# Seven-product groups in eight blocks of the mixers, and another order of pairs in the first down block

## The chip, the cores and the metric

The kernel runs on one core of one Trainium2 chip. TensorE (PE in the profile) multiplies matrices from on-chip memory (SBUF) into the accumulators (PSUM); VectorE (DVE) and ScalarE (ACT) prepare its operands and work on its results; SyncE (SP) issues most of the loads. The metric is the device time of one execution in microseconds (us), the median of several runs.

## The reference, cut to what matters

One decoder layer for 256 tokens of width 2048, all in fp32:

```
h = LN(alpha * x + 0.5 * swiglu(x, w_ffn1_gu, w_ffn1_down))
rq, rk, rv, rg, aq, ak, av, gate_r, gate_a = split(h @ w_in)
ro  = group_norm(retention(rotary(rq), rotary(rk), rv))
ret = (silu(rg) * ro) @ w_ret_out
att = sliding_window_attention(rotary(aq), rotary(ak), av, sinks) @ w_att_out
mixed = (sigmoid(gate_r) * ret + sigmoid(gate_a) * att) @ w_mix_out
h = LN(alpha * h + mixed)
h = LN(alpha * h + 0.5 * swiglu(h, w_ffn2_gu, w_ffn2_down))
out = LN(alpha * h + sigmoid(h @ w_ple_gate) * (p @ w_ple_proj))
```

`swiglu(x) = (silu(g) * u) @ w_down` with `g, u` the two halves of `x @ w_gu`; the inner width is 5632.

## The kernel before, in words

**Products.** Every fp32 operand is kept as a high part (fp32r, the copy of ScalarE) and a low part (the difference, by VectorE): `split`, L83. A product of two operands is three matmuls (L324 to L326): low by high, high by high, high by low. The 256 tokens are two halves t of 128; the weights come in pairs of 128-row slices (`Unit`, one pair p of one block b of 1024 columns, which are two halves c of 512). A **plain pair** ("P") is 2 slices x 2 token halves x 2 column halves, eight products and thus 24 matmuls of 512 columns. A group of seven (`Seven`, "S", L153) gets the same eight block products out of seven, 21 matmuls: it multiplies sums and differences of the blocks. For that VectorE and ScalarE make sums of the weight blocks (`u`, `hu`, `lu`) beside three of the blocks themselves (`hb`, `lb`), L166 to L191; `seven_forms` (L383) makes sums of the left operand's blocks once per input; and four of the seven products are gathered over all sevens of a block in two more PSUM tiles (`aux`, L365), which `seven_common` (L399) folds after the last seven into a tile `eve` that is then added to the sums in PSUM.

**Order.** TensorE, VectorE, ScalarE and the queue of SyncE each run in the order in which the program issues. `plan` lists all weight units in the order of use. A small planner keeps a model clock for TensorE and VectorE (`clock`, `spend`, `after`, L196 to L260) and issues loads and splits of coming units ahead of their use as far as a budget of slots allows: all working tiles share 23 slots (`SLOTS`), `weights(n)` (L260) says how many of them weights may take at that point. A plain unit takes one slot loaded, two more while it is made, two when made; a seven takes one, five more, and keeps four, until `done` (L256). Other work, as the attention's heads, is put in the list `side` and issued piece by piece between units by `run_side` (L267); `lazy` is the same for the rotary tables.

**Stages.** `ffn` (L665) runs the gate and up products in eleven blocks `f1g` (each with four or three sevens but the first), then two down blocks: `f1d` (first 1024 columns) and `f1e`. Its 22 pairs are two per group of four 128-row slices; groups 6 to 9 (`SEVEN_DOWN`) have their forms made. In the first down block all pairs come in the order 0 to 21, with sevens at 12, 14, 15, 16, 18 and 19 (`down_units`, L646; `before_unit` L760 converts the rows for coming groups). In the second, plain pairs and sevens alternate. `Norm` (L461) runs the layer norm in pieces between the last products of one stage (`held`) and the first of the next (`front`), as `EVENTS` lists them: c columns, m moments, s scale, t turn (transposes and split, L485). `mixers` (L852) runs blocks `w_rv` 0, the rotary features `rqk`, `w_rv` 1, `rg` 0 and 1, the features `aqk` and `av`, then `gr` 0 and 1, `ga` 0 and 1, then for each b `w_ret` and `w_att`, and last `w_mix` 0 and 1; all these blocks are plain. The retention's heads, two at a time, go through `side` in steps `ret1` (scores), `ret2` (products and statistics), `ret2b` (normalization and gate), `ret3` (transposes) and `ret3b` (split). The attention's heads do so in `att1`, `att1b`, `att1c`, `att2`, `att3`, in four steps each beside `gr` and `ga`.

Of the kernel before, what the change touches and what calls it, by code (L numbers as in the profile page):

```python
# [15 lines left out]
P = 128  # L16
# [24 lines left out]
SEVEN_BOTH = (7, 9)  # L41
# [11 lines left out]
        "a6": "c0 m0 s00", "b6": "t00 c1 m1 s10", "c4": "s01", "c6": "t10", "d1": "s11", "d4": "t01", "d7": "t11",  # L53
    },
    {
        "a6": "c0 m0 s00", "b6": "t00 c1 m1 s10", "c4": "s01", "c6": "t10", "d1": "s11", "d4": "t01", "d7": "t11",
# [9 lines left out]
def layer(ctx: ExitStack, tc: tile.TileContext, io):  # L66
# [200 lines left out]
    def run_side(n=1):  # L267
        for _ in range(n):
            if side:
                side.pop(0)()  # L270
        for _ in range(6):
            if lazy and next(lazy[0], "end") == "end":
                lazy.pop(0)
# [76 lines left out]
    def block(name, b, units, lhs, forms, sums, fold, before=None):  # L350
        sevens = [p for kind, p in units if kind == "S"]
        aux = None
        for j, (kind, p) in enumerate(units):
# [27 lines left out]
            run_side()  # L381
# [79 lines left out]
    class Norm:  # L461
# [23 lines left out]
        def turn(self, t, g):  # L485
# [18 lines left out]
        def vectors_and_p(self):  # L504
            self.vectors = ln_vectors(self.i)
            if self.i < 2:
                self.p = slot([P, 2, 512], F32R, "pt")
                split(self.p[:, :, :S], self.p[:, :, S:], p_raw)

        def held(self, name, b, ps, lhs):  # L510
            self.new = big.tile([P, KD, 512], F32R, tag="ht", name=f"ht{self.i}")
            us = [take(name, b, p) for p in ps]
            for j in range(2 * len(ps)):
                at = j % len(ps)
                some_products(us[at], ps[at], lhs, self.sums, (0,), (j // len(ps),))
                fill()
                run_side()
                self.at("a", j + 1)
# [61 lines left out]
    trig = []  # L580
# [14 lines left out]
    def rotary_tables():  # L595
# [6 lines left out]
        table = slot([P, 8, S], F32, "trig")  # L602
        trig.extend(table[:, j, :] for j in range(4))
        cos_r, sin_r, cos_a, sin_a = trig
        for inv, sgn, cos, sin, nm in ((0, 2, cos_r, sin_r, "r"), (1, 3, cos_a, sin_a, "a")):
# [25 lines left out]
            act.activation(cos, na, AF.Sin)  # L631
            yield
# [4 lines left out]

    def gu_units(j):
        if j == 0:
            return plain(PAIRS)  # L640
        order = "PPSSPSSP" if j % 2 else "PPSPSPSP"
        sevens = list(SEVEN[: order.count("S")])
        rest = [p for p in range(PAIRS) if p not in sevens]
        return [(kind, (sevens if kind == "S" else rest).pop(0)) for kind in order]

    def down_units():  # L646
        first = []
        for g in range(KF // 4):
            first += [("S" if g in SEVEN_DOWN else "P", 2 * g), ("S" if g in SEVEN_BOTH else "P", 2 * g + 1)]
# [15 lines left out]
    def ffn(name, i, ht, norm, keep, residual, keepers, away):  # L665
# [93 lines left out]

        def before_unit(u):  # L760
            g = u // 2 + 2
            others((KF // 4 + min(g, KF // 4 - 1) + 2) // 2 + (1 if u >= 10 else 0))
            if u % 2 == 0:
                if 2 <= u < 2 + 2 * len(SEVEN_DOWN):
                    at = u // 2 - 1
                    r = SEVEN_DOWN[at]
                    made[r] = seven_forms(raws[r // 2][:, r % 2 * 4 : r % 2 * 4 + 4], (space[:, 2 * at], space[:, 2 * at + 1]))
                if g < KF // 4:
                    convert(g)
# [16 lines left out]
        def before_unit(u):  # L786
            others(2 + (4 if u >= 12 else 0) + sum(at >= u for at in last.values()))
# [11 lines left out]
        norm.vectors_and_p()  # L799
        weights(SLOTS - (6 if i else 8))  # L800
# [22 lines left out]

    def plan_mixers():
        plan_block("w_rv", 0, plain(PAIRS))
        plan_features(range(8))
        plan_block("w_rv", 1, plain(PAIRS))
        for b in range(2):
            plan_block("rg", b, plain(PAIRS))
        plan_features(range(16, 21))  # L830
        plan.extend(Columns("w_av", c) for c in range(2))
        for name in ("gr", "ga"):
            for b in range(2):
                plan_block(name, b, plain(PAIRS))
        for b in range(2):
            plan_block("w_ret", b, plain(PAIRS))
            plan_block("w_att", b, plain(PAIRS // 2))
        for b in range(2):
            plan_block("w_mix", b, plain(PAIRS))

    def plain_block(name, b, lhs, n=PAIRS, start=0, sums=None):
        ps = None
        if sums is None:
            ps = [banks(f"{name}{b}{t}") for t in range(2)]
            sums = sums_of(by_half(ps), plain(n))
        block(name, b, plain(n)[start:], lhs, None, sums, None)
        return ps
# [4 lines left out]
    def mixers(ht, norm, residual, keepers, away):  # L852
# [4 lines left out]
        rv = []  # L857

        def values(b, ps):
            after()  # L860
            spend(1024)
            v = slot([P, 2, 1024], F32, f"rvs{b}")
            act.copy(v[:, 0], flat(ps[0]))
            dve.tensor_copy(v[:, 1], flat(ps[1]))
            rv.append(v)

        ps, sums = norm.front("w_rv", 0, rhs, plain(PAIRS))
        lazy.append(rotary_tables())
        plain_block("w_rv", 0, rhs, start=FRONT, sums=sums)
        values(0, ps)  # L870
        assert not lazy
        cos_r, sin_r, cos_a, sin_a = trig
        weights(8)
# [5 lines left out]
        decay = [slot([P, 4, 384], F32, f"dec{j}") for j in range(2)]  # L879
        for j in range(2):  # L880
            act.dma_start(decay[j], io["decay"][:, 4 * j : 4 * j + 4, :])
        values(1, plain_block("w_rv", 1, rhs))
# [5 lines left out]
        def ret1(i):  # L888
            def f():
# [5 lines left out]
                s = slot([P, 2, 384], F32, f"rsc{i}")  # L895
# [29 lines left out]
        def ret2b(i):  # L925
            def f():
# [3 lines left out]
                o = slot([P, 2, 2, DV], F32, f"ron{i}")  # L930
# [9 lines left out]
                keep["o", i] = o  # L940
# [13 lines left out]
        def ret3b(i):  # L954
            def f():
                ps = keep.pop(("r", i))
                ret_t[i] = slot([P, 4, 512], F32R, f"rett{i}")
                spend(256, 256, 256, 256)
                for x in range(4):
                    gk = gn[:, 4 * i + x : 4 * i + x + 1]  # L960
                    hi, lo = ret_t[i][:, x, :S], ret_t[i][:, x, S:]
                    act.mul(hi, ps[:, x], gk)
                    dve.scalar_tensor_tensor(lo, ps[:, x], gk, hi, ALU.mult, ALU.subtract)
            return f

        def gates(b, ps):
            g = slot([P, 2, 1024], F32, f"rgs{b}")
            for t in range(2):
                act.activation(g[:, t], flat(ps[t]), AF.Silu)
            gate.append(g)  # L970

        side.extend([idle] * 5 + [ret1(0), ret1(1), ret2(0)])
        gates(0, plain_block("rg", 0, rhs))
        steps = [
            (ret2b(0), ret2(1)), (ret3(0), ret2b(1)), (ret3b(0), ret3(1)), (ret3b(1),),
            (ret1(2),), (ret1(3),), (ret2(2),), (ret2(3),),
        ]
        both = lambda jobs: lambda: [f() for f in jobs]
        side.extend(both(jobs) for jobs in steps)
        gates(1, plain_block("rg", 1, rhs))  # L980
        side.extend(both(jobs) for jobs in [(ret2b(2),), (ret3(2), ret2b(3)), (ret3b(2), ret3(3)), (ret3b(3),)])
        aq, akv = slot([P, 8, S], F32, "aq"), slot([P, 4, S], F32, "akv")
# [111 lines left out]
        for m in range(8):  # L1094
            side.append(att1(m))
            side.append(both([att1b(m)] + ([att3(m - 1)] if m else [])))
            side.append(att1c(m))
            side.append(att2(m))
        sig = {}
        for name in ("gr", "ga"):  # L1100
            for b in range(2):
                if (name, b) == ("ga", 1):
                    run_side(1)
                ps = plain_block(name, b, rhs)
                sig[name, b] = slot([P, 2, 1024], F32, f"sig{name}{b}")
                for t in range(2):
                    act.copy(sig[name, b][:, t], flat(ps[t]))
        side.append(att3(7))
        run_side(len(side))
# [3 lines left out]

        def quarter(v):
            return lambda k: (v[k // 4][:, k % 4, :S], v[k // 4][:, k % 4, S:])
# [12 lines left out]
        for b in range(2):  # L1128
            pair = sig["gr", b], sig["ga", b]
            for v in pair:  # L1130
                act.activation(v, v, AF.Sigmoid)
            for v, name, n, a in ((pair[0], "w_ret", PAIRS, ret_t), (pair[1], "w_att", PAIRS // 2, att_t)):
                ps = plain_block(name, b, quarter(a), n)
                after()
                spend(1024, 1024)
                for t in range(2):
                    dve.tensor_tensor(v[:, t], v[:, t], flat(ps[t]), ALU.mult)
            v = pair[0]
            spend(1024, 1024)
# [237 lines left out]
```

## Time and profile before

| what | us |
|---|---|
| median of 3 runs | 2305.69 |
| lowest, highest run | 2305.38, 2306.9 |
| the profiled execution | 2308.07 |
| its span, first to last instruction | 2306.3 |

The profile is of one execution, whose own time is 2308.07 us. The page gives each engine's busy time, the chain of work that ended last, and the costliest groups of instructions with what ended the idle time ahead of them. In names of groups, `f1d<-hf_down,f1ac` means that the tile `f1d` is written from `hf_down` and `f1ac`. Matmuls overlap, so that their durations add up to more than TensorE's time.

### The profile page before, as it was taken

To read this page: it belongs to the slowest core of one execution; us is meant where nothing else is said; L and a number is where in the kernel's file an instruction comes from. 1 tells how busy PE (TensorE), PEld (TensorE's weight loads), DVE (VectorE), ACT (ScalarE), POOL (GpSimd) and SP (SyncE) were. 2 spreads that over 40 slices of the span, in tenths; PEclk is the share of its full clock that TensorE was granted. 3 is DMA by queue.
4 is the path that set the end of the run, shared out by engine and by line. 5 is a ranking of instruction groups with operands and counts; after the bars stand their busy time and mean duration, and the time that the engine had idled before them with its cause. 6 is when DMAs were issued, how large, how long until landed. Compare 5 with 4: busy or idle time off the path is not lost.

```text
span 2306.3 us, 26593 instructions
## 1 busy us (share of the span) xinstructions
PE 2275.3 (99%) x10490; PEld 1885.7 (82%) x10490; DVE 1802.4 (78%) x1571; ACT 1128.9 (49%) x922; POOL 0.7 (0%) x6
## 2 busy tenths in 40 slices
PE   8999999999999999999999999999999999999997
PEld 6888888888788888888777888878888888878876
DVE  6999898888988774567555555689989989889876
ACT  5555554555554343344444543356455456555541
POOL 0000000000000000000000000000000000000000
PEclk9999999999999999999999999999999999999999
DMA  8665565655577555445455656676656556455761
GB/s 311 206 199 187 192 209 183 201 201 183 219 262 279 189 201 192 146 164 186 161 164 172 211 201 224 212 238 201 201 179 222 183 175 232 159 205 214 287 261 55
DMA packets 227692, 465.31 MB, mean 202 GB/s; under 512 B 16624, under 2 KB 89072, under 8 KB 225008
## 3 DMA queue, kind: packets, MB, share of 16 engines
q1 hardware_dynamic: 225552, 459.86, 58.3%
q10 hardware_dynamic: 2016, 3.76, 0.5%
q8 instruction: 82, 1.34, 0.2%
q14 instruction: 42, 0.34, 0.0%
HBM read 455.17 MB, written 8.39 MB: 201 GB/s over the span
## 4 chain that ended last, share of the span: by engine, by line
PE 94%; DVE 3%; DMA 1%; issue 1%; ACT 0%; SPq 0%; DVEq 0%; ACTq 0%
PE f1g L326 5%; PE f1g L324 5%; PE f1g L325 5%; PE f2g L324 4%; PE f2g L325 4%; PE f2g L326 4%; PE rqk L288 3%; PE aqk L288 2%; PE f2d L324 1%; PE f2d L325 1%; PE f2d L326 1%; PE ga L324 1%; PE f1e L326 1%; PE f1e L325 1%; PE f1e L324 1%; PE gr L324 1%
## 5 line engine op out<-in xcount | busy, mean ns | idle before, releaser
L85 DVE TENSOR_TENSOR lf_gu<-rf_gu,hf_gu 128x2048 fp32r<-128x2048 f32 (+1 forms) x109 | 239.9, 2228 | 49.6 <-ACT hf_gu L84 48.9
L84 ACT CAST hf_gu<-rf_gu 128x2048 fp32r<-128x2048 f32 (+1 forms) x109 | 200.2, 1861 | 37.4 <-DMA rf_gu<-in_f_gu 15.6
L324 PE MATMUL f1g<-hf_gu,xt 128*128 128x512 f32 x424 | 166.7, 393 | 6.8 <-ACT hf_gu L84 6.4
L326 PE MATMUL f1g<-lf_gu,xt 128*128 128x512 f32 x424 | 166.4, 392 | 1.6 <-DVE lf_gu L85 1.6
L325 PE MATMUL f1g<-hf_gu,xt 128*128 128x512 f32 x424 | 166.4, 392 | 0.0
L188 DVE TENSOR_TENSOR luf_gu<-uf_gu,huf_gu 128x2048 fp32r<-128x2048 f32 x70 | 160.0, 2286 | 1.6
L85 DVE TENSOR_TENSOR lf_down<-rf_down,hf_down 128x2048 fp32r<-128x2048 f32 x60 | 136.4, 2288 | 25.1 <-ACT hf_down L84 18.2
L324 PE MATMUL f2g<-hf_gu,ht 128*128 128x512 f32 x360 | 140.1, 389 | 0.4 <-DVE eve L407 0.4
L326 PE MATMUL f2g<-lf_gu,ht 128*128 128x512 f32 x360 | 140.1, 389 | 0.0
L325 PE MATMUL f2g<-hf_gu,ht 128*128 128x512 f32 x360 | 140.1, 389 | 0.0
L176 ACT CAST huf_gu<-uf_gu 128x1024 fp32r<-128x1024 f32 x70 | 73.7, 1053 | 128.4 <-DVE uf_gu L175 103.4
L84 ACT CAST hf_down<-rf_down 128x2048 fp32r<-128x2048 f32 x60 | 113.8, 1910 | 44.0 <-DMA rf_down<-in_f_down 22.8
L185 DVE TENSOR_TENSOR lbf_gu<-rf_gu,hbf_gu 128x1536 fp32r<-128x1536 f32 x70 | 122.7, 1752 | 13.2 <-ACT hbf_gu L174 13.1
L174 ACT CAST hbf_gu<-rf_gu 128x1536 fp32r<-128x1536 f32 x70 | 103.5, 1479 | 22.3 <-DMA rf_gu<-in_f_gu 17.5
L324 PEld LDWEIGHTS f1g<-hf_gu,xt 128*128 128x128 f32 x424 | 80.5, 190 | 24.3 <-ACT hf_gu L84 6.8
L326 PEld LDWEIGHTS f1g<-lf_gu,xt 128*128 128x128 f32 x424 | 80.4, 190 | 19.0 <-DVE lf_gu L85 2.3
L325 PEld LDWEIGHTS f1g<-hf_gu,xt 128*128 128x128 f32 x424 | 80.3, 189 | 16.7
L175 DVE TENSOR_TENSOR uf_gu<-rf_gu 128x1024 f32<-128x1024 f32 x70 | 85.4, 1219 | 3.7 <-PE f1g L326 1.4
L181 ACT CAST huf_gu<-uf_gu 128x1024 fp32r<-128x1024 f32 x70 | 73.7, 1052 | 25.9 <-DVE uf_gu L180 25.9
L324 PEld LDWEIGHTS f2g<-hf_gu,ht 128*128 128x128 f32 x360 | 67.6, 188 | 14.9 <-issue 0.8
L326 PEld LDWEIGHTS f2g<-lf_gu,ht 128*128 128x128 f32 x360 | 67.6, 188 | 14.1
L727 ACT ACTIVATE eve<-eve 128x1024 f32<-128x1024 f32 x20 | 21.2, 1062 | 118.1 <-DVE eve L725 118.1
(938 smaller groups left out, 6071.9 us busy)
## 6 DMA issues: line engine op xcount, KB each, us to landing
rf_gu<-in_f_gu SPq DMA_DIRECT2D x210, 512.0 KB, 5.7
rf_down<-in_f_down SPq DMA_DIRECT2D x176, 512.0 KB, 4.5
rf_gu<-in_f_gu SPq DMA_DIRECT2D x280, 256.0 KB, 4.3
rw_rv<-in_w_rv SPq DMA_DIRECT2D x32, 512.0 KB, 4.5
rrg<-in_w_in_f SPq DMA_DIRECT2D x32, 512.0 KB, 4.9
rgr<-in_w_in_f SPq DMA_DIRECT2D x32, 512.0 KB, 4.6
rga<-in_w_in_f SPq DMA_DIRECT2D x32, 512.0 KB, 4.7
rw_ret<-in_w_ret SPq DMA_DIRECT2D x32, 512.0 KB, 4.7
```

The source lines that it names most:

```text
L84: act.copy(dst_hi, src)
L85: dve.tensor_tensor(dst_lo, src, dst_hi, ALU.subtract)
L174: act.copy(hb, raw[:, 1:])
L175: dve.tensor_tensor(u[:, 0:2], raw[:, 1:3], raw[:, 0:1].broadcast_to([P, 2, 512]), ALU.add)
L176: act.copy(hu[:, 0:2], u[:, 0:2])
L181: act.copy(hu[:, 2:], u[:, 2:])
L185: dve.tensor_tensor(lb, raw[:, 1:], hb, ALU.subtract)
L188: dve.tensor_tensor(lu, u, hu, ALU.subtract)
L288: pe.matmul(ps[:, f], u.tile_of(kk)[0][:, f * P : (f + 1) * P], rhs(k), start=k == 0, stop=k == KD - 1,)
L324: pe.matmul(o, al, bh, start=first, stop=False)
L325: pe.matmul(o, ah, bh, start=False, stop=False)
L326: pe.matmul(o, ah, bl, start=False, stop=self.left == 0)
```

## The change

- In the mixers eight blocks get sevens (`MIXERS`): four each in `w_rv` 1 and `rg` 0, three each in `gr` 0, `gr` 1, `w_ret` 0 and `w_ret` 1, two each in `w_mix` 0 and 1. `rg` 1, `ga`, `w_att` and `w_rv` 0 stay plain. The forms of the mixers' input come from a kept copy that the first norm now makes too; `ret3b` and `turned` write an fp32 copy first, from which high part, low part and forms are made.
- The blocks come in another order: `gr` 0, `w_ret` 0, `gr` 1, `w_ret` 1, `ga` 0, `ga` 1, `w_att` 0, `w_att` 1.
- The retention's steps of two heads are joined: `ret2` and `ret2b` in one, `ret3`, the next `ret1` and `ret3b` in one. The attention's heads take two steps each instead of four, beside `w_ret` 1 and `ga`.
- In the first down block of both half-FFNs the pairs come in another order (`FIRST_ORDER`), the same six sevens between plain pairs; rows of a group are converted up to five units ahead (`AHEAD`).
- In the norms the second half of the columns is turned earlier or later by one to two products (`EVENTS`), and the split reads PSUM directly, with the kept copy after it.
- Side work is not issued while a block's sevens are under way, and not after a block's last unit; budgets of slots change with all this.

```diff
+FIRST_ORDER = (0, 1, 2, 3, 4, 5, 6, 12, 7, 13, 14, 8, 15, 9, 16, 17, 10, 18, 11, 19, 20, 21)
+FIRST_SEVENS = (12, 14, 15, 16, 18, 19)
+AHEAD = 5
+MIXERS = {
+    ("w_rv", 1): ("PSPSPSSP", (0, 1, 2, 3)),
+    ("rg", 0): ("PSPSPSSP", (0, 1, 2, 3)),
+    ("gr", 0): ("PPSPSPSP", (0, 1, 2)),
+    ("gr", 1): ("PPSPSPSP", (0, 1, 2)),
+    ("w_ret", 0): ("PPSPSPSP", (0, 1, 2)),
+    ("w_ret", 1): ("PPSPSPSP", (0, 1, 2)),
+    ("w_mix", 0): ("PPPPSPSP", (4, 5)),
+    ("w_mix", 1): ("PSPSPPPP", (4, 5)),
+}
...
-        "a6": "c0 m0 s00", "b6": "t00 c1 m1 s10", "c4": "s01", "c6": "t10", "d1": "s11", "d4": "t01", "d7": "t11",
+        "a6": "c0 m0 s00", "b6": "t00 c1 m1 s10", "c5": "t10", "c6": "s01", "d1": "s11", "d4": "t01", "d5": "t11",
...
-                run_side()
+                if (aux is None or not sevens) and j < len(units) - 1:
+                    run_side()
...
-            if self.keep is not None and k0 < 8:
-                full = self.keep[:, k0 : k0 + nk, t * P : (t + 1) * P]
-                act.copy(full, ps)
-                ps = full
             dst = self.new[:, k0 : k0 + nk, :]
             split(dst[:, :, t * P : (t + 1) * P], dst[:, :, S + t * P : S + (t + 1) * P], ps)
+            if self.keep is not None and k0 < 8:
+                act.copy(self.keep[:, k0 : k0 + nk, t * P : (t + 1) * P], ps)
...
         def before_unit(u):
...
+            while todo and firsts[groups.index(todo[0])] <= u + AHEAD:
+                g = todo.pop(0)
+                if g in SEVEN_DOWN:
+                    at = SEVEN_DOWN.index(g)
+                    to = space[:, 2 * at], space[:, 2 * at + 1]
+                    made[g] = seven_forms(raws[g // 2][:, g % 2 * 4 : g % 2 * 4 + 4], to)
+                convert(g)
+            left = {g // 2 for g in todo}
+            others(len(left) + len(groups) - len(todo) + 1 + (1 if u >= 10 else 0))
...
+    def mixers_block(name, b, lhs, forms=None, n=PAIRS, fold=None):
+
+        ps = [banks(f"{name}{b}{t}") for t in range(2)]
+        units = mixers_units(name, b, n)
+        got = []
+        block(name, b, units, lhs, forms, sums_of(by_half(ps), units), lambda *a: got.append((fold or seven_common)(*a)))
+        return ps, got[0] if got else None
+
+    def joined(ps, e, name):
+        if e is None:
+            v = slot([P, 2, 1024], F32, name)
+            for t in range(2):
+                act.copy(v[:, t], flat(ps[t]))
+            return v
+        v = e.rearrange("p (t c) n -> p t (c n)", t=2)
+        after()
+        spend(1024, 1024)
+        for t in range(2):
+            dve.tensor_tensor(v[:, t], v[:, t], flat(ps[t]), ALU.add)
+        return v
...
+            if grp == 4:
+                to = [slot([P, 16, P], F32R, f"hf{w}") for w in "hl"]
+                made["x"] = seven_forms(norm.keep, to)
...
+        def retention(j):
+            i = 2 * j
+            side.append(ret1(i))
+            side.append(both(ret2(i), ret2b(i)))
+            side.append(both(ret3(i), ret1(i + 1), ret3b(i)))
+            side.append(both(ret2(i + 1), ret2b(i + 1)))
+            side.append(both(ret3(i + 1), ret3b(i + 1)))
+            if not j:
+                side.append(retention_forms)
+        weights(10)
+        for b in range(2):
+            load_decay(b)
+            ps, e = mixers_block("rg", b, rhs, forms)
+            v = joined(ps, e, f"rgs{b}")
+            act.activation(v, v, AF.Silu)
+            gate.append(v)
+            retention(b)
+            weights(7)
...
+        weights(8)
+        of_ret = lambda p: made["r"](p)
+        branch = {}
+        for b in range(2):
+            sig = joined(*mixers_block("gr", b, rhs, forms), f"sigr{b}")
+            act.activation(sig, sig, AF.Sigmoid)
+            if b:
+                side.append(both(att1(0), att1b(0)))
+                side.append(att1c(0))
+            ps, e = mixers_block("w_ret", b, quarter(ret_t), of_ret)
+            after()
...
+        for m in range(1, 8):
+            side.append(both(att2(m - 1), att1(m), att1b(m)))
+            side.append(both(att3(m - 1), att1c(m)))
+        side.append(att2(7))
         side.append(att3(7))
-        run_side(len(side))
+        sig = [joined(*mixers_block("ga", b, rhs, forms), f"siga{b}") for b in range(2)]
+        run_side(len(side) - 1)
+        for v in sig:
+            act.activation(v, v, AF.Sigmoid)
...
+            g = 2 * b + hf
+            raw = slot([P, 4, S], F32, f"mixr{g}")
+            act.copy(raw, ps)
             after(clock["pe"] + 1.2)
             spend(1024)
-            split(mt[:, :, :S], mt[:, :, S:], ps)
+            split(mt[:, :, :S], mt[:, :, S:], raw)
+            if any(2 * g in MIXERS[key][1] for key in MIXERS if key[0] == "w_mix"):
+                hl = slot([P, 2, 8, P], F32R, f"mixf{g}")
+                made["m", g] = seven_forms(raw, (hl[:, 0], hl[:, 1]))
```

More of the change, by code (lines that the diff above doesn't have):

```diff
@@ L517, in held @@
                 run_side()
+                if j == 1 and self.i < 2:
+                    self.p = slot([P, 2, 512], F32R, "pt")
+                    split(self.p[:, :, :S], self.p[:, :, S:], p_raw)
                 self.at("a", j + 1)
@@ L636, in plain, with in_order @@
         return [("P", p) for p in range(n)]
+    def in_order(order, sevens):
+        rest = [p for p in range(PAIRS) if p not in sevens]
+        sevens = list(sevens)
+        return [(kind, (sevens if kind == "S" else rest).pop(0)) for kind in order]
     def gu_units(j):
@@ L641, in gu_units @@
         order = "PPSSPSSP" if j % 2 else "PPSPSPSP"
-        sevens = list(SEVEN[: order.count("S")])
-        rest = [p for p in range(PAIRS) if p not in sevens]
-        return [(kind, (sevens if kind == "S" else rest).pop(0)) for kind in order]
+        return in_order(order, SEVEN[: order.count("S")])
     def down_units():
-        first = []
-        for g in range(KF // 4):
-            first += [("S" if g in SEVEN_DOWN else "P", 2 * g), ("S" if g in SEVEN_BOTH else "P", 2 * g + 1)]
+        first = [("S" if p in FIRST_SEVENS else "P", p) for p in FIRST_ORDER]
         rest = [p for p in range(KF // 2) if p // 2 not in SEVEN_DOWN]
@@ L822, in plan_features, with mixers_units, blocks @@
         plan.extend(Columns("f", (grp, c)) for grp in grps for c in range(2))
+    def mixers_units(name, b, n=PAIRS):
+        return in_order(*MIXERS[name, b]) if (name, b) in MIXERS else plain(n)
     def plan_mixers():
-        plan_block("w_rv", 0, plain(PAIRS))
+        def blocks(*which):
+            for name, b in which:
+                plan_block(name, b, mixers_units(name, b, PAIRS // 2 if name == "w_att" else PAIRS))
+        blocks(("w_rv", 0))
         plan_features(range(8))
-        plan_block("w_rv", 1, plain(PAIRS))
-        for b in range(2):
-            plan_block("rg", b, plain(PAIRS))
+        blocks(("w_rv", 1), ("rg", 0), ("rg", 1))
         plan_features(range(16, 21))
         plan.extend(Columns("w_av", c) for c in range(2))
[L832 to L847, printed above, removed]
+        blocks(("gr", 0), ("w_ret", 0), ("gr", 1), ("w_ret", 1), ("ga", 0), ("ga", 1))
+        blocks(("w_att", 0), ("w_att", 1), ("w_mix", 0), ("w_mix", 1))
+    def mixers_block(name, b, lhs, forms=None, n=PAIRS, fold=None):
[16 more added lines that the diff above has]
+        return v
     def flat(ps):
@@ L855, in mixers @@
         both_halves = lambda k: ht[:, k, :]
[L857 to L865, printed above, removed]
+        made = {}
+        forms = lambda p: made["x"](p)
         ps, sums = norm.front("w_rv", 0, rhs, plain(PAIRS))
         lazy.append(rotary_tables())
-        plain_block("w_rv", 0, rhs, start=FRONT, sums=sums)
-        values(0, ps)
-        assert not lazy
+        block("w_rv", 0, plain(PAIRS)[FRONT:], rhs, None, sums, None)
+        rv = [joined(ps, None, "rvs0")]
+        assert "r" in trig_done
         cos_r, sin_r, cos_a, sin_a = trig
-        weights(8)
+        weights(12)
         rq, rk = (slot([P, 8, S], F32, f"r{w}") for w in "qk")
@@ L877, in mixers @@
             features_out(grp, both_halves, ps)
+            if grp == 4:
+                to = [slot([P, 16, P], F32R, f"hf{w}") for w in "hl"]
+                made["x"] = seven_forms(norm.keep, to)
             rotate(ps, f"rr{grp}", (rq, rk)[grp // 4][:, grp % 4 * 2 : grp % 4 * 2 + 2, :], cos_r, sin_r, SH_R)
[L879 to L882, printed above, removed]
+        weights(11)
+        rv.append(joined(*mixers_block("w_rv", 1, rhs, forms), "rvs1"))
         ret_t = {}
@@ L929, in f @@
                 rsqrt(rs, mv[:, :, 1], 4, GN_EPS)
-                o = slot([P, 2, 2, DV], F32, f"ron{i}")
+                o = keep["o", i]
                 spend(*[0] * 10, 256, 256, 256, 256)
@@ L964, in ret3b @@
-            return f
[L966 to L982, printed above, removed]
+                    act.mul(raw[:, x], ps[:, x], gn[:, 4 * i + x : 4 * i + x + 1])
+                after(clock["pe"] + 2)
+                spend(1024)
+                split(ret_t[i][:, :, :S], ret_t[i][:, :, S:], raw)
@@ new lines, in f, with load_decay, retention_forms @@
+                if i == 1:
+                    keep["full"] = keep["raw"]
+            return f
+        both = lambda *jobs: lambda: [f() for f in jobs]
+        decay = []
+        def load_decay(j):
+            decay.append(slot([P, 4, 384], F32, f"dec{j}"))
+            act.dma_start(decay[j], io["decay"][:, 4 * j : 4 * j + 4, :])
+        def retention_forms():
+            to = [slot([P, 16, P], F32R, f"retf{w}") for w in "hl"]
+            made["r"] = seven_forms(keep.pop("full"), to)
@@ L1159, in mixers @@
         ps = [banks(f"mo1{t}") for t in range(2)]
-        sums = sums_of(by_half(ps), plain(PAIRS))
-        plain_block("w_mix", 1, lhs, PAIRS - HELD, sums=sums)
-        norm = Norm(ps, sums, combine, y, stats, 1, LN_EPS, keepers, away)
-        norm.vectors_and_p()
-        weights(15)
-        norm.held("w_mix", 1, range(PAIRS - HELD, PAIRS), lhs)
+        units = mixers_units("w_mix", 1)
+        held = [p for kind, p in units[-HELD:]]
+        sevens = any(kind == "S" for kind, p in units)
+        sums = sums_of(by_half(ps), units)
+        block("w_mix", 1, units[:-HELD], lhs, of_mix, sums, fold(1))
+        norm = Norm(ps, sums, add if sevens else combine, y, stats, 1, LN_EPS, keepers, away)
+        norm.load_vectors()
+        weights(13)
+        norm.held("w_mix", 1, held, lhs)
         return norm
@@ L1194, in embedding @@
         sg = slot([P, 2, 1024], F32, "sg0")
-        plain_block("w_pg", 0, lhs, start=FRONT, sums=sums)
+        block("w_pg", 0, plain(PAIRS)[FRONT:], lhs, None, sums, None)
         whole = slice(0, 1024)
```

112 lines of the change are left out of this document (52 added, 60 removed).

## The prediction, as it was put on record

> **What bounds the kernel now.** I read the page first, then the waits of TensorE, then the stages, then single rows.
>
> ```profile
> span 2306.3 us, 26593 instructions
> PE 2275.3 (99%) x10490; PEld 1885.7 (82%) x10490; DVE 1802.4 (78%) x1571; ACT 1128.9 (49%) x922; POOL 0.7 (0%) x6
> ...
> PE 94%; DVE 3%; DMA 1%; issue 1%; ACT 0%; SPq 0%; DVEq 0%; ACTq 0%
> ```
>
> TensorE is busy for 99% of the span and makes 94% of the chain that ended last. Only fewer matmuls, or fewer of its few waits, can shorten this kernel. The waits of TensorE that touch the change:
>
> ```profile
> PE f_down0s L326 <- DVE luf_down L188: 2.5, 2, 1.2
> PE f_down0s L326 <- DVE lbf_down L185: 2.4, 2, 1.2
> PE f_gu L324 <- DVE ht L85: 1.6, 2, 0.9
> ```
>
> The first two are in the first down blocks (one per half-FFN), the third is where the mixers' norm hands over to the second FFN. A busy TensorE hides the price of one matmul, because starts overlap; so I take it from first and last starts.
>
> ```profile
> L324 PE MATMUL mo<-hw_mix,mixt x64: 389/389/389, 1444.5 to 1487.4; 128*128 128x512 f32 x64
> L326 PE MATMUL mo<-lw_mix,mixt x64: 389/389/393, 1445.0 to 1487.8; 128*128 128x512 f32 x64
> ```
>
> Those 192 matmuls start 191 steps apart over 1487.8 - 1444.5 = 43.3 us: **0.2267 us a matmul**. A plain pair is 24 of them (5.44 us), a seven 21 (4.76 us). The FFN's blocks, which have sevens already, confirm it:
>
> ```profile
> 66.71 0.87 PE f1t L681 x8
> 108.41 0.87 PE f1t L681 x8
> 150.78 0.87 PE f1t L681 x8
> ```
>
> 41.70 us is 180 matmuls (four sevens) plus 0.87 of transposes; 42.37 us is 183 (three) plus 0.87. So a block with sevens has run at TensorE's own pace. By stages (columns: window, length, then busy PE, PEld, DVE, ACT, POOL, clock, DMA):
>
> ```profile
> 60.00:476.70 416.70, 416.31 (x1878) 345.24 (x1877) 379.10 (x275) 229.15 (x179) 0.00 (x0) 1.00 0.62 201
> 476.70:596.50 119.80, 117.32 (x520) 96.38 (x519) 99.06 (x81) 64.41 (x49) 0.00 (x0) 1.00 0.48 171
> 596.50:716.70 120.20, 120.20 (x536) 99.61 (x535) 111.43 (x88) 61.91 (x44) 0.00 (x0) 1.00 0.71 260
> 716.70:853.00 136.30, 136.30 (x734) 118.05 (x733) 101.83 (x122) 53.01 (x40) 0.00 (x0) 1.00 0.57 209
> 853.00:1000.00 147.00, 147.00 (x668) 122.58 (x667) 78.50 (x95) 57.46 (x47) 0.00 (x0) 1.00 0.54 178
> 1000.00:1069.50 69.50, 69.50 (x436) 62.83 (x435) 55.59 (x86) 35.33 (x36) 0.00 (x0) 1.00 0.52 182
> 1069.50:1266.70 197.20, 197.17 (x947) 156.02 (x945) 107.63 (x143) 89.48 (x132) 0.00 (x0) 1.00 0.50 166
> 1266.70:1399.20 132.50, 132.50 (x594) 109.86 (x593) 67.79 (x37) 60.36 (x36) 0.00 (x0) 1.00 0.62 214
> 1399.20:1487.80 88.60, 88.60 (x400) 73.54 (x399) 54.54 (x44) 30.73 (x18) 0.00 (x0) 1.00 0.62 217
> ```
>
> In the FFN, VectorE is 91% busy (379.10 of 416.70) and TensorE loses 0.39 us: that much VectorE work is bearable. The mixers (last six rows) have no TensorE gap to remove, but VectorE is busy for only 465.9 of 771.1 us. That is the room for the new work.
>
> **The change part by part.**
>
> *Sevens in the mixers.* 4+4+3+3+3+3+2+2 = 24 pairs become sevens, each 3 matmuls less: 72 x 0.2267 = **-16.3 us**. The Trainium skill, page "TensorE: Matmul & The Clock Gate", section "Wait — 56ns, not 53.3ns?", has warm N=512 matmuls start 215.7 ns apart; by it the term would be -15.5. The trace has 226.7 ns, and the trace is used.
>
> VectorE pays. One seven, and the plain pair behind it:
>
> ```profile
> 525.53 1.22 DVE L175 TENSOR_TENSOR uf_down<-rf_down 128x1024 f32<-128x1024 f32 x1
> 526.78 0.69 DVE L179 TENSOR_TENSOR uf_down<-rf_down,uf_down 128x512 f32<-128x512 f32 x1
> ...
> 528.12 1.75 DVE L185 TENSOR_TENSOR lbf_down<-rf_down,hbf_down 128x1536 fp32r<-128x1536 f32 x1
> 529.78 2.28 DVE L188 TENSOR_TENSOR luf_down<-uf_down,huf_down 128x2048 fp32r<-128x2048 f32 x1
> 532.01 2.29 DVE L85 TENSOR_TENSOR lf_down<-rf_down,hf_down 128x2048 fp32r<-128x2048 f32 x1
> ...
> 592.98 0.68 DVE L405 TENSOR_TENSOR eve<-eve,f_down0s 128x512 f32<-128x512 f32 x1
> ...
> 594.41 1.22 DVE L407 TENSOR_TENSOR eve<-f_down0s,eve 128x1024 f32<-128x1024 f32 x1
> ```
>
> A seven takes 532.01 - 525.53 = 6.48, a plain pair 2.29: 4.19 more, x24 = 100.6. Each of the eight blocks folds its four common products once (592.98 to 595.63, 2.65): 21. Joining fold and sums is two 1024-wide additions (2 x 1.22, as L407) in six blocks, one of which had a copy: 13; a 2048-wide combine (2.29) in two: 5. Two whole-input forms are four 1024-wide operations and one of 2048 (4 x 1.22 + 2.28 = 7.2): 14; the mix form about 3 (1.22 and four narrow ones). ret3b's sixteen narrow operations become four of 1024: nothing. In all some 157: 465.9 + 157 = 623 of about 755 us, 82%, below the FFN's 91%. So on average TensorE covers this; if the cover went, 157 us would be in the path. ScalarE copies what VectorE subtracts; with as much again (101) on its 326.4 busy it stays under 60%. The 16 grouped sevens load in four DMAs, not two of double the size: the FFN's do so too. The other order of blocks moves loads and matmuls but adds none, and w_ret's rows are ready before the gr blocks. The decay loads move past the features on ScalarE's queue and are used a block later: nothing.
>
> Locally it is tight. Blocks w_rv 1 and rg 0 have four sevens: 4 x 6.48 + 4 x 2.29 + 2.65 + 2.44 = 40.2 of VectorE beside 180 x 0.2267 = 40.8, twice running, without the three-seven block between that relieves the FFN; and the last rotation (five 512-wide operations, 5 x 0.69 as L179) spills in. From w_mix 0's first seven to w_mix 1's last, four sevens and four plain pairs, fold, combine and the norm's sums and statistics (2 x 1.22 and 4 x 0.69 if they run like L407 and L179) are 45 beside 40.8. Three plain pairs made ahead would cover 7 us. I take **+2** (0 to +10).
>
> *Retention.* Before, head products (ret2), normalization (ret2b) and transposes (ret3) stood in three successive side steps; now ret2 and ret2b share one, so one pair, not two, lies between products and transposes. The chain, as it ran:
>
> ```profile
> 942.01 0.59 PE L913 MATMUL ro<-rvs,rsc 128*128 128x256 f32 x2
> ...
> 944.80 0.43 DVE L920 BATCH_NORM_STATS2 gst<-ro 128x6 f32<-128x256 f32 x1 [4.93 <-PE ro L915]
> ...
> 946.87 0.18 DVE L921 BATCH_NORM_AGGREGATE gmv<-gst 128x2 f32<-128x6 f32 x1
> ...
> 949.18 0.16 DVE L413 SCALAR_TENSOR_TENSOR nv<-gmv,cst 128x8 f32<-128x8 f32 x1
> ...
> 951.05 1.65 DVE L936 SCALAR_TENSOR_TENSOR ron<-ro,gmv,rgs 128x256 f32<-128x256 f32 x4
> ...
> 951.56 1.71 ACT L939 ACTIVATE ron<-ron,grs 128x256 f32<-128x256 f32 x4 [6.54 <-DVE ron L936]
> ```
>
> Products and hand-over 2.79, statistics 2.25 (944.80 to 947.05), square root 1.87 (949.18 to 951.05), scaling on both engines 2.22 (951.05 to 953.27): 9.13 us. TensorE is back after about 2.7 of products and one pair of 5.44: 8.1. It waits 1.0 us for each of four head pairs (I take the same for the two in the aqk stage). A busy VectorE queue adds up to one plain split (2.29) each; transposes that may start on the first head save half. Behind TensorE's wait stand the next pair's matmuls and, behind them, the loads into the slots that they free. I take **+4** (0 to +14).
>
> *Room.* Slots for weights are 7 to 8 of 23 around gr, w_ret and ga, and a seven needs 6 at once. I take **+2** (0 to +24, the slower rival below).
>
> *First down blocks.* Their sevens stay six; they are spread between plain pairs. From first start to last:
>
> ```profile
> L324 PE MATMUL f1d<-hf_down,f1ac x128: 389/389/476, 476.7 to 595.7; 128*128 128x512 f32 x128
> L324 PE MATMUL f2d<-hf_down,f2ac x128: 389/389/476, 1963.8 to 2083.9; 128*128 128x512 f32 x128
> ...
> 2068.60 0.80 PE L326 MATMUL f_down0s<-luf_down,f2forms 128*128 128x512 f32 x1 [1.24 <-DVE luf_down L188]
> 2069.19 0.63 PE L324 MATMUL f_down0s<-huf_down,f2forms 128*128 128x512 f32 x1
> 2069.62 0.63 PE L325 MATMUL f_down0s<-huf_down,f2forms 128*128 128x512 f32 x1
> ```
>
> With three more matmuls of 0.2267 the blocks last 119.7 and 120.8; 16 x 24 + 6 x 21 = 510 matmuls and 0.87 of transposes are 116.5. So 3.2 and 4.3 us are to be had. The second down block (third stage row) alternates sevens and plain pairs already and has no gap, with VectorE at 93%; that speaks for the new order. What is late next: slots fall from 10 or 11 to 9, and a last seven's pieces must be made within one plain pair. I keep 1 us of stall in each: **-5.5** (-7.5 to 0).
>
> In the second block a gap of 1.24 us was followed by matmuls 0.43 us apart, half pace. That is a risk for every new stall: about six slow matmuls, 6 x 0.2 = 1.2 us. The Trainium skill, same page, section "HAM oscillation — how this bites in real kernels", gives as the rule to avoid idle gaps over about 3.4 us. This trace disagrees once, at 1.24 us; by the rule retention's short waits could not slow the clock, and its upper end would be about 5 us lower.
>
> *Norms.* In the mixers' norm the second half is now turned two steps earlier and split straight from PSUM, the kept copy after it: of 1.6 us waited I take **-0.8** (-1.6 to +1.5, if the earlier t10 finds its scaling late). The first norm's four extra copies lie on ScalarE (53.01 of 136.30 busy there): nothing, at most 1. Attention's side steps, halved in number, keep a pair between steps; ga stays plain: 0, at most +2.
>
> **The sum.** -16.3 + 2 + 4 + 2 - 5.5 - 0.8 = **-14.6**. Against the profiled execution (2308.07, of which the span is 2306.3) that is 2293.5; the profiled time is 2.4 above the median of the shown runs, so against the median 2305.69 it is **2291 us** (-0.6%).
>
> **The rivals.**
>
> *All new work hidden* (0.17): -16.3 - 7.5 - 1.6 = -25.4, **2280**. For it: FFN blocks at 91% VectorE without stalls. Against: retention's 9.13 beside 8.1.
>
> *VectorE or retention becomes the bound in places* (0.13): upper ends, +10 and +10, in place of +2 and +4: -0.6, **2305**. It decides once the pairs made ahead are used up, thus in rg 0 and w_mix 1; against it, the plain blocks rg 1 and ga.
>
> *Slots chain the loads* (0.11): slower. If other tiles fill the remaining 15 slots, the plain pair after a seven is loaded only into a slot that this seven frees. Then from the end of the seven before:
>
> ```profile
> L174 ACT CAST hbf_gu<-rf_gu 128x1536 fp32r<-128x1536 f32 x70 | 103.5, 1479 | 22.3 <-DMA rf_gu<-in_f_gu 17.5
> ...
> rw_ret<-in_w_ret SPq DMA_DIRECT2D x32, 512.0 KB, 4.7
> ```
>
> 1.48 + 1.75 (L185) + 4.7 (load) + 2.0 (high part, 1.48 x 2048 / 1536) + 2.29 (low part) = 12.2, against 5.44 + 4.76 + 0.45 = 10.65 of matmuls; with hand-overs 2 us late for each of twelve sevens in gr and w_ret: +24 in place of +2, **2313**. Against it: I count 10 to 14 such tiles there (forms, retention's rows, aq, tables, gates), so one to five slots are spare.
>
> The change certainly does what it says of matmuls; no rival there.
>
> **How the numbers follow.** Forecast 0.59, its own range 2284 to 2299. Range for 8 in 10: **2278 to 2306**, from the hidden case to the VectorE case; left out are the slot chain and a tail below. About 0.2% (4.6 us) is what a measurement can tell from no change: faster (below 2301) 0.59 + 0.17 + 0.05 = 0.81; same, the rest of the VectorE case, 0.08; slower 0.11.
>
> **What would show it.** Matmul records fall by 72 (in the trace 10490 to about 10418). New waits of TensorE: rt on ron (about 1 us each, four times), few on lb or lu rows of rg, w_rv and w_mix. The first down blocks last 117 to 118. VectorE's busy time rises to about 1950. I am wrong if TensorE waits for weight pieces of gr or w_ret over 1 us at each seven (slots), or if the span falls by under 10 with none of these waits.

## The result, and the profile after

The changed kernel took 2288.69 us (median of 4 runs, 2287.03 to 2291.25), the kernel before 2306.3 (4 runs, 2305.38 to 2310.07): a ratio of 0.9922, 95% interval 0.9904 to 0.9939, thus 14 to 22 us. The forecast was 2291. The profiled execution took 2287.03 us, 21.0 less than that of before.

The page after, in the lines that answer to those of before:

```profile
span 2285.2 us, 26799 instructions
PE 2257.9 (99%) x10418; PEld 1871.4 (82%) x10418; DVE 1947.1 (85%) x1704; ACT 1184.9 (52%) x988; POOL 0.7 (0%) x6
...
PE 92%; DVE 5%; ACT 1%; DMA 1%; issue 1%; SPq 0%; DVEq 0%; ACTq 0%
```

There are 72 matmuls less (10490 to 10418) and 145 us more of VectorE's work (1802.4 to 1947.1), and TensorE is as busy as before. What TensorE still waits for (total, times, longest):

```profile
PE f1g L341 <- ACT hf_gu L101: 5.9, 1, 5.9
PE f1g L343 <- DVE lf_gu L102: 1.6, 1, 1.6
PE at L1112 <- DVE asc L1102: 1.3, 1, 1.3
PE lnps L509 <- issue: 0.8, 1, 0.8
PE mo L343 <- DVE lw_mix L102: 0.8, 1, 0.8
...
PE ga L341 <- DVE eve L425: 0.4, 1, 0.4
...
PE f_gu L343 <- DVE lf_gu L102: 0.3, 1, 0.3
```

The waits for lbf_down and luf_down are gone and the wait for ht is gone; new are `at` (attention's transposes), `mo` (w_mix 1) and `ga`. Where the time went, by stages. Each number is the distance from the first matmul of a tile to the first of the next one named, out of the tile views:

| stretch | before | after | difference |
|---|---|---|---|
| start to f1d | 476.7 | 475.2 | -1.5 |
| f1d (first down block) | 119.7 | 116.5 | -3.2 |
| f1e, first norm, w_rv 0 | 166.8 | 166.8 | 0.0 |
| rqk, w_rv 1, rg | 237.2 | 225.2 | -12.0 |
| aqk, av | 69.1 | 78.2 | +9.1 |
| gr, w_ret, ga, w_att | 329.7 | 324.0 | -5.7 |
| w_mix 0 | 45.3 | 43.9 | -1.4 |
| mo (w_mix 1), mixers' norm | 49.9 | 49.6 | -0.3 |
| f_gu (second FFN's first pairs) | 48.4 | 46.7 | -1.7 |
| f2g | 421.0 | 421.0 | 0.0 |
| f2d (first down block) | 120.8 | 116.5 | -4.3 |
| f2e to the end | 221.7 | 221.6 | -0.1 |

The rows rqk and aqk belong together: half of the retention's heads moved from the one to the other. The first row lies ahead of all that the change edits, and it is the clock: behind a wait of 1.59 us at 16.3 us the granted clock of the kernel before is 0.50 (18 to 20 us), while behind an equal wait at 16.4 us that of the changed kernel is 1.00. The other run that has the mixers of before (`down_alone`) has the low clock there too, the runs below that edit the changed kernel have not; why was not tried.

### The profile page after: what moved, and what is told of

It is laid out like the page before. It is cut to its first block, busy times and chain, and to the rows that moved or that the text cites. A ratio compares the mean times of both kernels' runs of the same rounds, so it can differ in the third digit from the quotient of the medians.

```text
span 2285.2 us, 26799 instructions
## 1 busy us (share of the span) xinstructions
PE 2257.9 (99%) x10418; PEld 1871.4 (82%) x10418; DVE 1947.1 (85%) x1704; ACT 1184.9 (52%) x988; POOL 0.7 (0%) x6
## 4 chain that ended last, share of the span: by engine, by line
PE 92%; DVE 5%; ACT 1%; DMA 1%; issue 1%; SPq 0%; DVEq 0%; ACTq 0%
PE f1g L343 5%; PE f1g L341 5%; PE f1g L342 5%; PE f2g L341 4%; PE f2g L342 4%; PE f2g L343 4%; PE rqk L305 3%; PE f1d L343 1%; PE f2d L341 1%; PE f1d L342 1%; PE f2d L343 1%; PE f2d L342 1%; PE f1d L341 1%; PE f1e L343 1%; PE f1e L342 1%; PE f1e L341 1%
## 5 line engine op out<-in xcount | busy, mean ns | idle before, releaser
L202 DVE TENSOR_TENSOR lbf_gu<-rf_gu,hbf_gu 128x1536 fp32r<-128x1536 f32 x70 | 122.6, 1751 | 12.3 <-ACT hbf_gu L191 12.3
```

Source lines behind the costliest of these rows:

```text
L202: dve.tensor_tensor(lb, raw[:, 1:], hb, ALU.subtract)
```

## The experiments

Each is an edit of the changed kernel, but for `down_alone`, which edits the kernel before. "Ratio" is to the kernel before on the same chip, with its 95% interval.

**The changed kernel again (after_again).**

> The changed kernel once more, as the measure for the other runs of this call. Both theories: 2287 to 2291 us, span near 2286.

2288.24 us (2287.13 to 2289.03), ratio 0.9917 (0.9902 to 0.9932). The runs below are compared with this median; only no_sevens, old_order and ret_apart ran on the same chip, so for the others the ratios and the stages say more than a difference of medians.

**All blocks of the mixers plain (no_sevens).**

```diff
-MIXERS = {
...
+MIXERS = {}
```

> The changed kernel with plain pairs in all eight blocks of the mixers; order of blocks, joined steps of the heads and first down blocks stay. Theory (each matmul counts 0.2267 us because TensorE never leaves the path): 72 matmuls come back, +16.3 us, less the about 1 us of waits that VectorE's extra work causes (lw_mix, eve), so 2303 to 2306. Rival (the sevens pay only part, the rest of the gain being order and norms): +8 to +12, 2297 to 2301.

2299.56 us (2299.31 to 2300.78), ratio 0.9966 (0.9954 to 0.9977): 11.3 us more than the changed kernel, which is in the rival's range and not in the theory's. (The forms of the mixers' input and of the retention's rows are still made in this run.) The stages say where the rest of the 16.3 goes. From this run to the changed kernel, first starts again: rqk to rg 132.6 to 129.8, rg 98.1 to 95.4, gr 0 43.5 to 41.5, w_ret to ga 131.7 to 126.1, ga 107.4 to 109.9, w_mix 0 45.3 to 43.9, mo 49.8 to 49.6. Four sevens give 2.7 us, three in gr 0 give 2.0 and two in w_mix 0 give 1.4, as 0.68 each would have it; the nine of w_ret 0, gr 1 and w_ret 1 together give 5.6 of 6.1; and 2.5 us are lost in `ga`, which has no seven. All in all 12.2 of 16.3 arrive: 2.5 go in ga, 1.1 in w_mix 1, 0.5 from w_ret 0 to w_ret 1. In the profile of after_again the stretch w_ret to ga is 127.7 in place of 126.1, as w_ret 1 waits there 0.6 and 0.4 us for the fold of gr 1 to empty its PSUM tiles; against that execution 10.7 arrive. So what the sevens lose there varies from one execution to the next.

The chain of the changed kernel into ga (start, us, what), and VectorE's own queue there:

```profile
1214.45 9.90 DMA rga<-in_w_in_f
...
1224.45 1.93 ACT hga L101
1226.40 2.29 DVE lga L102
1228.69 0.61 DVE eve L423
```

```profile
1223.74 2.29 DVE L102 TENSOR_TENSOR lga<-rga,hga 128x2048 fp32r<-128x2048 f32 x1 [1.51 <-ACT hga L101]
1226.40 2.29 DVE L102 TENSOR_TENSOR lga<-rga,hga 128x2048 fp32r<-128x2048 f32 x1 [0.36 <-ACT hga L101]
1228.61 0.68 DVE L423 TENSOR_TENSOR eve<-eve,w_ret1s 128x512 f32<-128x512 f32 x1
...
1250.37 1.00 DVE L1102 TENSOR_SCALAR asc<-asc,asm 128x128 f32<-128x128 f32 x4
```

ga's loads are issued in a burst behind w_ret 1's sevens, and this one takes 9.9 us to land, where 4.7 was the median of such loads before. VectorE works in order: two splits of ga that wait for their loads (1.51 and 0.36 us behind ScalarE's copies) stand ahead of the fold of w_ret 1 (L423), so the fold, the gate and the attention's scores all run late, until TensorE waits 1.3 us for `asc` at 1250. This part of the sevens' price is thus paid not where they are multiplied but where VectorE next meets a chain with little slack; `slots9` below tests the late load.

**The old order of pairs (old_order).**

```diff
-FIRST_ORDER = (0, 1, 2, 3, 4, 5, 6, 12, 7, 13, 14, 8, 15, 9, 16, 17, 10, 18, 11, 19, 20, 21)
+FIRST_ORDER = tuple(range(22))
```

> The changed kernel with the pairs of the first down blocks in the order 0 to 21 again, sevens at 12, 14, 15, 16, 18, 19; conversions five units ahead as in the change. Theory (two sevens in a row ask 13 us of VectorE within 9.5 us of TensorE): the waits for lbf_down and luf_down come back, 3 to 4 us in each half-FFN, 2294 to 2298, first down blocks 119 to 121 us. Rival (the earlier conversions removed the waits, not the order): 2288 to 2291, first down blocks 116.5.

2300.39 us (2298.24 to 2303.37), ratio 0.997 (0.996 to 0.998): 12.2 us more, beyond the range that the theory gave. f1d lasts 121.6 and f2d 123.1, longer than before the change (119.7, 120.8). Its waits:

```profile
PE f_down0s L343 <- DVE lbf_down L202: 6.0, 4, 2.4
PE f_down0s L343 <- DVE luf_down L205: 1.7, 2, 1.2
```

The order it is, not the earlier conversions. The budget of slots there is smaller after the change; whether that makes the old order worse than it was, was not tried by itself.

**The new order alone (down_alone).** In the kernel before: `FIRST_ORDER`, `FIRST_SEVENS`, `AHEAD` and the first `before_unit` of the change, nothing else.

> The kernel before with nothing but the new order of pairs in the first down blocks (and its conversions and budgets). Theory: both blocks come down to 116.5 us as in the changed kernel, 3.2 and 4.3 us less, so 2298 to 2300 beside 2306 to 2308. Rival (the blocks gain only together with the other changes): 2303 or more.

2300.74 us (2298.89 to 2301.43), ratio 0.9964 (0.995 to 0.9978); f1d 116.5, f2d 116.4. The whole 7.6 us of the two blocks come from the new order with its conversions and budgets, without help from the rest of the change; old_order shows that without the order the conversions don't give them.

**Alternation at the end (late_alt).**

```diff
-FIRST_ORDER = (0, 1, 2, 3, 4, 5, 6, 12, 7, 13, 14, 8, 15, 9, 16, 17, 10, 18, 11, 19, 20, 21)
+FIRST_ORDER = (0, 1, 2, 3, 4, 5, 6, 7, 8, 9, 12, 10, 14, 11, 15, 13, 16, 17, 18, 20, 19, 21)
```

> The changed kernel with another order in the first down blocks: sevens and plain pairs alternate as strictly, but from the eleventh place on (0 to 9, then 12, 10, 14, 11, 15, 13, 16, 17, 18, 20, 19, 21), so that the last seven comes second to last. Theory (alternation is what counts, a seven and a plain pair ask 8.8 us of VectorE beside 10.2): waits under 1 us a block, blocks near 117. Rival (the early start counts, since conversions and the fold come on top): waits of 2 us or more for lbf or luf, blocks 118.5 to 121.

2301.46 us (2300.24 to 2303.59), ratio 0.9973 (0.996 to 0.9986). Neither was right. The waits:

```profile
PE f2e L341 <- DVE eve L423: 3.3, 1, 3.3
PE f1e L341 <- DVE eve L423: 2.6, 1, 2.6
PE f_down1s L343 <- DVE lbf_down L202: 1.7, 2, 1.3
```

Within the first down block no seven waits any more, so alternation does cure that. But with the last seven next to last, VectorE reaches the fold (L423) too late: the second block needs the PSUM tiles that the fold empties, and starts 2.6 and 3.3 us late; f1d becomes 119.7 and f2d 120.4 (116.5 in the changed kernel), and f1e 123.2 (120.6), where a seven waits 1.3 us for lbf_down too. So plain pairs behind the last seven are part of what the new order gives; it has two there and late_alt one, and no other number was tried.

**The retention's steps apart (ret_apart).**

```diff
-            side.append(both(ret2(i), ret2b(i)))
-            side.append(both(ret3(i), ret1(i + 1), ret3b(i)))
-            side.append(both(ret2(i + 1), ret2b(i + 1)))
-            side.append(both(ret3(i + 1), ret3b(i + 1)))
+            side.append(both(ret2(i), ret1(i + 1)))
+            side.append(both(ret2b(i), ret2(i + 1)))
+            side.append(both(ret3(i), ret2b(i + 1)))
+            side.append(both(ret3b(i), ret3(i + 1)))
+            side.append(ret3b(i + 1))
```

> The changed kernel with the retention's products, normalization and transposes in three side steps again, two pairs of heads interleaved as before the change. Theory: the transposes rt find their rows ready, their eight run 0.87 us instead of 1.6 to 1.7, so 4 x 0.75 = 3 us less: 2284 to 2287. Rival (the late rows cost nothing, because the group is only drawn out while TensorE has other matmuls): no change, 2287 to 2291.

2286.02 us (2285.19 to 2286.76), ratio 0.9908 (0.9891 to 0.9924): 2.2 us less than the changed kernel. rg goes from 95.4 to 94.0, aqk from 78.2 to 77.6: 2.0 of it. What the joined steps did, in the changed kernel:

```profile
944.17 0.43 DVE L950 BATCH_NORM_STATS2 gst<-ro 128x6 f32<-128x256 f32 x1 [3.69 <-PE ro L945]
...
946.45 0.17 DVE L431 SCALAR_TENSOR_TENSOR nv<-gmv,cst 128x8 f32<-128x8 f32 x1
...
948.32 1.65 DVE L966 SCALAR_TENSOR_TENSOR ret<-ro,gmv,eve 128x256 f32<-128x256 f32 x4
```

```profile
949.47 1.67 PE L979 MATMUL rt<-ident,ret 128*128 128x128 f32 x8
```

ScalarE's scaling in the chain of the changed kernel (start, us, what):

```profile
948.83 1.72 ACT ret L969 x4
```

and eight such transposes before the change, in the same view as the 1.67:

```profile
958.18 1.03 PE L950 MATMUL rt<-ident,ron 128*128 128x128 f32 x8
```

No wait of PE is listed for them, since the eight are drawn out (1.67 in place of 1.03) as ScalarE delivers the rows one by one; the weight loads show it:

```profile
PEld rt L979 <- ACT ret L969: 2.4, 10, 0.3
```

The 0.87 of the expectation is the length of the group in the chain that ended last, a view that leaves out the tail of the last transpose, so the 3 us were counted too high. In the one view the four groups take 1.67, 1.68, 1.59 and 1.75 where they took 1.03, or 1.04, before: 2.6 us in all. ret_apart gives 2.0 of them back and not all, because its last group waits for VectorE's rows:

```profile
PE rt L979 <- DVE ret L966: 0.6, 1, 0.6
```

**A slot more, a slot less (slots9, slots7).** `weights(8)` ahead of gr becomes `weights(9)` or `weights(7)`.

> The changed kernel with weights(9) in place of weights(8) ahead of gr, w_ret and ga. Theory (at the start of ga the first load is late because the budget holds it back, VectorE then makes the new pairs ahead of the fold, and the attention's first transposes wait): the load lands earlier, the waits of ga and at (1.7 us together, 2.5 with what follows) mostly go, 2285 to 2288. Rival (VectorE's total work in w_ret 1 is the cause, whatever the loads do): no change, 2287 to 2291.

2286.61 us (2285.46 to 2287.03), ratio 0.9903 (0.9888 to 0.9917): 1.6 less, on another chip and with ratios whose intervals overlap. The stage decides: ga is 109.9 or 110.0 in each run of the changed kernel that keeps `weights(8)`, no_sevens apart, and 107.8 here and in apart_slots9, and the waits of ga and at are gone. The two splits of ga ahead of the fold no longer wait for their loads. The expectation held.

> The changed kernel with weights(7) there. The slot chain of the prediction (a pair after a seven is loaded only into what the seven frees) should now show: about 2 us late for up to twelve sevens in gr and w_ret, 2300 to 2313. Rival (free slots beyond the budget hide it): 2288 to 2292.

2287.32 us (2 runs), ratio 0.9907 (0.9887 to 0.9926): no slot chain, and 0.7 us below the rival's range. One seven, the first of w_ret 1, waits:

```profile
PE w_ret1s L343 <- DVE luw_ret L205: 1.2, 1, 1.2
...
PE w_ret1s L343 <- DVE lbw_ret L202: 1.1, 1, 1.1
```

The stretch w_ret to ga is 129.0 (126.1 in the changed kernel), but ga is 107.4 (109.9): the later loads of ga let the fold pass. So the wait only changes its place, and the other eleven of the twelve sevens wait for no piece of their weights even with a slot less.

**The old order of norm pieces (old_events).**

```diff
-        "a6": "c0 m0 s00", "b6": "t00 c1 m1 s10", "c5": "t10", "c6": "s01", "d1": "s11", "d4": "t01", "d5": "t11",
+        "a6": "c0 m0 s00", "b6": "t00 c1 m1 s10", "c4": "s01", "c6": "t10", "d1": "s11", "d4": "t01", "d7": "t11",
```

> The changed kernel with the order of norm pieces of before (s01 at c4, t10 at c6, t11 at d7), while the split still reads PSUM and the kept copy comes after it. Theory (the wait at the second FFN's start came from the turn that stood two products later): TensorE waits again 0.8 to 1.6 us for ht in f_gu, and the stretch from the first f_gu matmul to f2g's is 47.5 to 48.4 us instead of 46.8. Rival (reading PSUM directly was what helped): it stays 46.8.

One run, 2292.18 us, span 2290.4 (5.2 more than the changed kernel's profile):

```profile
PE w_rv L341 <- DVE ht L102: 2.2, 1, 2.2
...
PE f_gu L341 <- DVE ht L102: 1.1, 1, 1.1
PE f_gu L343 <- DVE lf_gu L102: 1.1, 2, 0.8
```

The stretch f_gu is 49.3, more than expected and more than before the change (48.4); so reading PSUM directly is not, by itself, what helped. And w_rv 0, which had no gap before, goes from 46.2 to 48.7. There TensorE waits for ht, and VectorE's queue shows for what:

```profile
734.76 4.48 DVE L102 TENSOR_TENSOR lw_rv<-rw_rv,hw_rv 128x2048 fp32r<-128x2048 f32 x2
739.16 1.22 DVE L102 TENSOR_TENSOR ht<-lnps,ht 128x1024 fp32r<-128x1024 f32 x1
```

Two weight splits stand ahead of the low part of the last rows, whose high part ScalarE had ready at 736.6; before the change, one split stood there. The kept copies (L513 on ScalarE), which are new in this norm, end at 724.85 and are not what it waits for at that point. Why the planner puts two splits there was not tried.

**Both repairs (apart_slots9).**

> The changed kernel with both repairs: the retention's three steps apart (ret_apart) and weights(9) ahead of gr, w_ret and ga (slots9). Theory (the two waits lie in different stages and add): the changed kernel less about 1.9 and 2.1 us, a span near 2282, 2283 to 2286 us. Rival (one of the two was scatter between runs): 2286 to 2288.

2284.78 us (2282.89 to 2285.14, 4 runs), ratio 0.9899 (0.9883 to 0.9916), profiled span 2280.8, as expected. The median is the lowest of all kernels here; rg 94.0, aqk 77.6, ga 107.8, so the two add as the stages say. Its interval and that of the changed kernel overlap, but its slowest run lies below the changed kernel's fastest (2287.03).

## Why the prediction was right, point by point

- **TensorE bounds, 0.2267 us a matmul.** Right: blocks with sevens are shorter by 0.68 us a seven (2.7 for four, 2.0 for three), and the second FFN's gate and up blocks, which had sevens before, did not move (f2g 421.0).
- **Sevens -16.3, VectorE +2, room +2.** The sum of the three was -12.3; 12.2 arrived in one profile, 10.7 in another, 11.3 in the medians. That it fits so closely is partly luck, since the costs were not where I put them. w_rv 1 and rg 0, which I held for the tightest, lost nothing. ga, which I put at 0 and at most +2, lost 2.5, by late loads and the order of VectorE's queue; a slot more gives 2.1 of it back, so this was a price of room, but not by the path that I gave it. w_mix 1 lost 1.1, where VectorE does fold and combine ahead of a plain split, in the stretch for which I had counted 45 us beside 40.8. VectorE's work grew by 145 us; the forecast was 157. Of the difference 4.3 are the two whole-input forms, whose four sums are 512 wide (0.69 us each) and not 1024 (1.22). The rival of the slot chain did not come, not even with a slot less.
- **Retention +4.** The chain was right to some hundredths: from the first products at 941.38 to the last scaled row at 950.55 are 9.17 us (forecast 9.13), TensorE was back 8.09 after (8.1). The wait of 1.0 us a pair that I concluded from it did not come, since the eight transposes begin as rows arrive; each group is drawn out by some 0.64 instead. That is 2.6 us for the four by the rows, and 2.5 by the stages (rqk to gr: 308.8 in no_sevens, 306.3 before). The prediction named the early start and did not take it.
- **First down blocks -5.5.** -7.5: nothing was left of the gaps, since both blocks are at the 116.5 of their matmuls. I kept 1 us in each for the smaller budget; it has no price in this order. Of the stall that I read as a gap of 1.24 us I had left out that one of 1.13 stands 2.2 us ahead of it, and that the first half-FFN has the like pair (1.25 and 1.24) with no slow matmul behind.
- **Norms -0.8.** -1.7 at the second FFN. That the extra copies of the first norm (two, not four) cost nothing came out so with the new order of pieces; the prediction took copies and order for separate terms, and with the old order the stretch w_rv 0 is 2.5 us longer, by VectorE's queue and, as far as its rows show, not by the copies.
- **The sum.** -14.6 forecast, -21.0 in the profiled executions, of which 1.5 lie ahead of all that was changed; -17.6 in the medians. The remainder in the profiles is the down blocks (2.0), retention (1.5), the norm (0.9) and the other blocks and steps of gr to w_att (0.6, from 329.7 before to 329.1 in no_sevens). Of the terms, sizes and places were off, no sign.

## What to carry to other kernels

Where a block already runs at the pace of its matmuls, a saved matmul is worth its full pitch, and the price of the preparation is to be sought in the next stage whose chain on the preparing engine has little slack, not only in the block itself. When costly and cheap units share an engine in order, alternate them, and keep enough cheap ones behind the last costly one for the work that closes the block. A wait that is drawn out over many short instructions is not listed as a wait; compare the length of the group with that of before, in the same view.

## What the runs showed of the hardware that was not expected

Two gaps of the same length had different consequences. In old_order TensorE stood for 2.35 us in the first half-FFN and for 2.38 in the second, at the same place in the block:

```profile
566.76 0.50 PE L343 MATMUL f_down0s<-lbf_down,f1ac 128*128 128x512 f32 x1 [2.35 <-DVE lbf_down L202]
```

```profile
2046.39 0.80 PE L343 MATMUL f_down0s<-lbf_down,f2ac 128*128 128x512 f32 x1 [2.38 <-DVE lbf_down L202]
2046.98 0.63 PE L341 MATMUL f2d<-hbf_down,f2ac 128*128 128x512 f32 x1
2047.40 0.63 PE L342 MATMUL f2d<-hbf_down,f2ac 128*128 128x512 f32 x1
```

After the second the next matmuls start 0.43 us apart in place of 0.23 until 2049.5; after the first they do not. The granted clock (last column but two) says the same, 1.00 behind the first gap and 0.50 behind the second:

```profile
566.70:569.30 2.60, 2.54 (x11) 1.91 (x11) 2.60 (x3) 2.60 (x2) 0.00 (x0) 1.00 0.10 39
2046.40:2049.60 3.20, 3.20 (x8) 2.55 (x9) 3.20 (x2) 2.52 (x2) 0.00 (x0) 0.50 0.06 20
```

The other traces agree that the length of the gap alone does not decide it. In late_alt the clock is 1.00 behind a gap of 2.63 us and 0.52 behind one of 3.32; in the kernel before it is 0.51 behind the 1.24 in the second half-FFN and 1.00 behind the 1.24 in the first. The Trainium skill, page "TensorE: Matmul & The Clock Gate", section "What's actually happening", says that activity is judged in a window that runs on its own and does not follow the kernel; that would let equal gaps end differently. No run here shows the window itself, and these gaps are shorter than the 3.4 us that the page gives.
